# First FFN of a diffusion layer: up product once over 1280 tokens in chunks of 512, 512 and 256, the gated features by way of DRAM to a down product in two blocks

## The chip, the cores and the metric

The kernel runs on one core of one Trainium2 chip. The metric is the device time of one execution in microseconds (us). TensorE (PE in the profile; PEld is its weight load) multiplies, VectorE (DVE) and ScalarE (ACT) do elementwise work, GpSimd (POOL) does nearly nothing here, and SyncE (SP) issues the transfers between DRAM and the on-chip memory (SBUF).

## The reference

One layer over 1024 latent and 256 context tokens, width 1024: a half-step SwiGLU FFN, a mixer (neighbourhood attention and a state-space scan, S5), and a second half-step FFN. The change is in the first FFN, which both token streams go through with the same weights:

```python
mod = jnp.split((jax.nn.silu(c) @ w_ada[layer] + b_ada[layer])[:, None, :], 9, axis=-1)
...
def swiglu(h, w_up, w_down):
    a, g = jnp.split(h @ w_up, 2, axis=-1)
    return (jax.nn.silu(g) * a) @ w_down
...
x = post_norm(x, 0.5 * mod[2] * swiglu(modulate(x, mod[0], mod[1]), ffn1_w_up[layer], ffn1_w_down[layer]),
              ln_g[layer, 0], ln_b[layer, 0])
h_c = post_norm(h_c, 0.5 * mod_c[2] * swiglu(modulate(h_c, mod_c[0], mod_c[1]),
                                             ffn1_w_up[layer], ffn1_w_down[layer]),
                ln_g[layer, 0], ln_b[layer, 0])
```

D_FF is 2816, that is 22 features of 128 (the code's `NF`); the up weights are 44 units (a and g for each feature), the down weights 22.

## The kernel before

Each product keeps float32 accuracy by splitting both operands into a high part that TensorE takes exactly and a rest. `mm3` (L337 to L339) then makes three matmuls of one: high by high, high by low, low by high. Weights are loaded as 512 KB units (`ws`, L221), and each half of a unit is split by ACT (`wh`, L259) and DVE (`wl`, L261) into a ring of four.

The first FFN takes the 1280 tokens in two blocks of 640, b = 0 and 1, the second half latent and half context (384 latent, 256 context). Each block is done in two halves h of 11 features. In a half `ffn_up` makes the 11 hidden features: for each unit `by_feature` runs over two chunks of tokens, 384 and 256, with eight k-steps of three matmuls in each, into a PSUM bank per chunk. `gate` multiplies a by silu(g) (L365 silu on ACT, L366 product on DVE) and splits the result into high (L367) and low (L368, put off to the next `flush`). The hidden features stay in SBUF (`HA`, `HB`). `token_major` then makes the down product: features by five token tiles by three matmuls of 512 columns (L397 to L399), twice for the two halves of the output's 1024 columns; its `evac` adds the result, times a gate row, to the residual tile (L610, L611). So the up and the down weights are loaded and split once for each block.

The head of the program loads the modulation weights, builds the modulated input `X` (high and low, L526) eight k-slices one after the other, and `grow` already computes the first four units on each slice as it comes in. After a block the layer norm runs: statistics (L420), scaling (L436), and a store of each normed tile to a DRAM array, `xh` (L624), which `xm_a` later reads back (`z`, L1008) and transposes on TensorE (L450) as input of the mixer. For block 0 this transposing lies in the up and down products of block 1.

The order within an engine is that in which the program issues. `pump` lets generators of side work (preparation of S5, the modulation rest `mods_rest`, normed rows) advance a few us at a time between products. SP issues its transfers strictly in order, so one that has to wait holds back those behind it.

Of the kernel before, what the change touches and what calls it, by code (L numbers as in the profile page):

```python
# [38 lines left out]
NHX = 2368  # L39
TAIL = 8  # L40
# [8 lines left out]
def hybrid_layer(ctx: ExitStack, tc: tile.TileContext, I, out, dbg=None, stop=99):  # L49
# [67 lines left out]
    def ztile():  # L117
        return work.tile([128, 1024], F32, name=nm("z"), tag="z", bufs=4)
# [19 lines left out]
    ffn = lambda i: [I[f"w{p}{i}"][h * n + j] for h in range(2) for p, n in (("u", NF), ("d", NF // 2)) for j in range(n)]  # L138
# [52 lines left out]
    plain(ffn(1) * 2 + col("wu", 4) + wv[:2] + col("wu", 4) + wv[2:] + wv)  # L191
# [8 lines left out]
    for f, i in ORDER:  # L200
        item(*sv[f][i])
    DOWN = len(items)
    plain(col("wd2", NF) + [I["wd2"][f:f + 2, :, h * 512:(h + 1) * 512].rearrange("f p c -> p f c")
                            for h in range(2) for f in range(0, NF, 2)])
# [90 lines left out]
    early = slott("HA", [128, 16 * NB])  # L295
    mod_room = [early[:, i * 1024:(i + 1) * 1024] for i in range(10)]
# [72 lines left out]

    def ffn_up(X, chunks, hid, us, started=()):  # L370
        part = lambda f, c: [hid(i, f)[:, chunks[c][0]:sum(chunks[c])] for i in range(2)]
        for f, (a, g) in enumerate(started):
            for c in range(len(chunks)):
                flush()
                gate(a[c], g[c], *part(f, c))
        for f in range(len(started), NF // 2):
            a = by_feature(take(2), X, chunks, "m", lambda c, p: (pump(us), flush()))
            by_feature(take(2), X, chunks, "m", lambda c, p: (pump(us), flush(), gate(a[c], p, *part(f, c))))
        flush()
# [104 lines left out]
    def x_block(m=KD, n=NB):  # L484
# [3 lines left out]
    CH = ((0, 384), (384, 256))  # L488
    X = x_block()
    room = slott("HX", [128, NHX], F32R)  # L490
    room = [slott(f"A{i}", [128, 1024], F32R) for i in range(5)] + [room[:, 0:1024], room[:, 1024:2048],
                                                                   rowt().bitcast(F32R)]
    for i in range(8):
        apart[i] = room[i][:, 0:512], room[i][:, 512:1024]
    pb8 = [[bank("s")[:, :n] for _, n in CH] for _ in range(4)]
# [12 lines left out]
    for k in range(KD):  # L508
# [16 lines left out]
        S.activation(X[0][k], xt, AF.Copy)  # L525
        rest_of = lambda k=k, xt=xt: V.tensor_tensor(X[1][k], xt, X[0][k].bitcast(F32), op=ALU.subtract)  # L526
# [16 lines left out]
    def mods_rest():  # L543
        todo = [(m, k, lat, cx) for m, lat, cx in
                ((2, 1, 1), (0, 0, 1), (1, 0, 1), (3, 1, 1), (4, 1, 1), (5, 1, 0), (6, 1, 0), (7, 1, 0), (8, 1, 0))
                for k in range(KD)]
        hx = slott("HX", [128, NHX])
        mod_room[:] = [xe[:, 2, :], xe[:, 3, :], hx[:, 0:1024], hx[:, 1024:2048]]
        ws = [mod_load(*t[:2]) for t in todo[:4]]
        yield None  # L550
        for i, (m, k, lat, cx) in enumerate(todo):
            mod_tile(ws.pop(0), m, k, lat, cx)
            if i + 4 < len(todo):
                ws.append(mod_load(*todo[i + 4][:2]))
            yield 1.35 * (lat + cx)
            if (m, k) == (2, KD - 1):
# [6 lines left out]
        V.tensor_tensor(modc[:, 0:2, :], modc[:, 0:2, :], bada[:, 0:2, :], op=ALU.add)  # L563
# [12 lines left out]
    def x_build(X):  # L576
        for k in range(0, KD, 2):
            zs = [ztile()[:, 0:NB] for i in range(2)]
            for i in range(2):
                dq.dma_start(zs[i], I["xT"][k + i, :, NB:2 * NB])  # L580
            yield None
            yield None
            for i in range(2):
                j = k + i
                z = zs[i]
                S.activation(z[:, 0:384], z[:, 0:384], AF.Identity, scale=modl[:, 1, j:j + 1], bias=modl[:, 0, j:j + 1])
                S.activation(z[:, 384:NB], z[:, 384:NB], AF.Identity, scale=modc[:, 1, j:j + 1],
                             bias=modc[:, 0, j:j + 1])
                split(X[0][j], X[1][j], z)
                yield 0.8  # L590


    def ffn(X, chunks, zs, gates, us, done, last=None, scale=1.0, affine=None, started=()):
        N = chunks[-1][0] + chunks[-1][1]
        nt = N // 128
        for h in range(2):
            ha, hb = slott("HA", [128, 16 * NB], F32R), slott("HB", [128, 6 * NB], F32R)

            def hid(i, f):
                n = i * (NF // 2) + f  # L600
                t, n = (ha, n) if n < 16 else (hb, n - 16)
                return t[:, n * N:(n + 1) * N]

            ffn_up(X, chunks, hid, us[0], started if h == 0 else ())
            if h == 1 and last is not None:
                last()

            def evac(hf, t, p):
                z = zs[t][:, hf * 512:(hf + 1) * 512]
                V.tensor_tensor(p, p, gates(t)[:, hf * 512:(hf + 1) * 512], op=ALU.mult)  # L610
                V.scalar_tensor_tensor(z, z, scale if h == 0 else 1.0, p, op0=ALU.mult, op1=ALU.add)  # L611
                if h:
                    half_done(t, hf, z)

            half_done, rest = norm(affine)
            token_major(NF // 2, nt, lambda f, t: (hid(0, f)[:, t * 128:(t + 1) * 128],
                                                   hid(1, f)[:, t * 128:(t + 1) * 128]), evac, us[1],
                        (2, 2) if h == 0 or affine is None else (2, TAIL))
        if affine is None:
            hi.append(rest(zs, done))  # L620
# [397 lines left out]
    zn = []  # L1018
    hi.append(rows_in(zn, I["xt"], 5))
    for b in range(2):  # L1020
        zs, zn = zn, []

        def nxt():
            if b == 0:
                Xn.append(x_block())
                hi.append(x_build(Xn[0]))
            else:
                drain(bg)
                hi.append(xm_a())

        Xn = []
        ffn(X, CH, zs, lambda t: rows["g2c" if b == 1 and t >= 3 else "g2"], ((2.2, 2.4), (2.4, 2.4))[b], ln1_done(5 * b),
            last=nxt, scale=ALPHA, started=started if b == 0 else ())
        if b == 0:
            hi.append(rows_in(zn, I["xt"][5:10], 5))
            X = Xn[0]
# [791 lines left out]
def layout(inp):  # L1828
# [15 lines left out]
    for i in (1, 2):  # L1844
        w = a[f"ffn{i}_w_up"][0].reshape(KD, 128, 2, NF, 128)
        r[f"wu{i}"] = asc(w.transpose(3, 2, 1, 0, 4).reshape(2 * NF, 128, 1024))
        w = a[f"ffn{i}_w_down"][0].reshape(2, NF // 2, 128, 2, 512).transpose(0, 3, 1, 2, 4)
        r[f"wd{i}"] = asc(w.reshape(NF, 2, 128, 512).transpose(0, 2, 1, 3).reshape(NF, 128, 1024))
    r["wd2"] = asc(a["ffn2_w_down"][0].reshape(NF, 128, 1024))
# [49 lines left out]
```

## Time and profile before

| what | value |
| --- | --- |
| median of three runs | 2208.72 us (2207.69 to 2210.64) |
| the profiled execution: its own time, its span | 2211.69 us, 2209.6 us |
| mean granted TensorE clock | 0.994 |
| PE busy | 2154.9 us (98%) |
| DVE busy | 1597.0 us (72%) |
| ACT busy | 739.1 us (33%) |
| bytes moved | 372.31 MB, mean 169 GB/s |

The profile is of one execution, and its own time is 3.0 us above the median. The first FFN takes about the first 967 us of the span. "Granted clock" is the share of TensorE's full clock that the chip allowed it.

### The profile page before, as it was taken

The numbers are of one execution on the slowest core, as the hardware profiler recorded it, in microseconds if no ns is written. First come the engines' busy times: TensorE is split into PE (matmuls) and PEld (weight loads), VectorE is DVE, ScalarE is ACT, GpSimd is POOL, SyncE is SP. The second block draws the span as 40 slices with busy tenths as digits, with TensorE's granted clock in tenths as the row PEclk, the third lists the DMA queues.
The fourth block names the chain that finished last, engine by engine and source line by source line (L and its number), as shares of the span: only waits on it lengthen the run. The fifth ranks groups of instructions, "written<-read, shape, count | busy, mean of one in ns | idle before, by whom it ended". The sixth has DMA issues, their size and how long they took to land. (4 is left out here: it accounts for less than half of the span.)

```text
span 2209.6 us, 32479 instructions
## 1 busy us (share of the span) xinstructions
PE 2154.9 (98%) x12272; PEld 1933.3 (87%) x12272; DVE 1597.0 (72%) x3425; ACT 739.1 (33%) x1547; POOL 22.0 (1%) x33
## 2 busy tenths in 40 slices
PE   6999999999999999999999999999899999999998
PEld 6998899889998999898899899986688888888786
DVE  7888878798887887553777466788877777744845
ACT  4322223423322223324222367634433333332121
POOL 0000000000000000000000000000000000000000
PEclk9999999999999999999999999999999999999999
DMA  9787723436433444433877675244223333279442
GB/s 353 251 291 258 268 67 109 161 100 237 128 124 117 126 135 128 137 125 128 274 252 248 179 175 136 81 168 162 103 108 114 115 114 115 96 266 390 168 150 83
DMA packets 169612, 372.31 MB, mean 169 GB/s; under 512 B 18152, under 2 KB 85736, under 8 KB 166640
## 3 DMA queue, kind: packets, MB, share of 16 engines
q1 hardware_dynamic: 169456, 370.25, 49.6%
q8 instruction: 96, 1.57, 0.3%
q14 instruction: 60, 0.49, 0.1%
HBM read 292.09 MB, written 84.06 MB: 170 GB/s over the span
## 5 line engine op out<-in xcount | busy, mean ns | idle before, releaser
L337 PE MATMUL pb<-X,wh 128*128 128x256 f32 (+2 forms) x1744 | 558.2, 320 | 0.9 <-ACT wh L259 0.9
L339 PE MATMUL pb<-X,wl 128*128 128x256 f32 (+2 forms) x1744 | 555.8, 319 | 0.0
L261 DVE TENSOR_TENSOR wl<-ws,wh 128x512 fp32r<-128x512 f32 x456 | 304.1, 688 | 246.8 <-ACT wh L259 241.3
L259 ACT ACTIVATE wh<-ws 128x512 fp32r<-128x512 f32 x456 | 278.7, 627 | 563.3 <-PE pb L399 288.0
L337 PEld LDWEIGHTS pb<-X,wh 128*128 128x128 f32 x1744 | 330.7, 190 | 9.6 <-ACT wh L259 1.3
L339 PEld LDWEIGHTS pb<-X,wl 128*128 128x128 f32 x1744 | 330.4, 189 | 8.7 <-DVE wl L261 0.4
L338 PE MATMUL pb<-X,wh 128*128 128x256 f32 (+2 forms) x946 | 306.8, 324 | 0.0
L338 PE MATMUL pb<-XT,wh 128*128 128x256 f32 (+2 forms) x886 | 283.3, 320 | 0.9 <-DVE XT L134 0.9
L397 PE MATMUL pb<-wh,HA 128*128 128x512 f32 x592 | 232.4, 393 | 2.0 <-DVE hid L366 1.4
L398 PE MATMUL pb<-wl,HA 128*128 128x512 f32 x592 | 230.5, 389 | 0.8 <-DVE wl L261 0.8
L338 PEld LDWEIGHTS pb<-X,wh 128*128 128x128 f32 x946 | 179.1, 189 | 7.1
L338 PEld LDWEIGHTS pb<-XT,wh 128*128 128x128 f32 x886 | 168.1, 190 | 6.4 <-DVE XT L134 1.8
L337 PE MATMUL pb<-HA,wh 128*128 128x512 f32 (+2 forms) x424 | 154.1, 364 | 0.6 <-ACT wh L259 0.6
L339 PE MATMUL pb<-HA,wl 128*128 128x512 f32 (+2 forms) x424 | 153.0, 361 | 0.0
L1642 DVE TENSOR_TENSOR z<-pb,z 128x512 f32<-128x512 f32 x154 | 106.1, 690 | 47.2 <-PE pb L339 43.8
L397 PEld LDWEIGHTS pb<-wh,HA 128*128 128x128 f32 x592 | 111.2, 188 | 26.0 <-DVE hid L366 2.3
L398 PEld LDWEIGHTS pb<-wl,HA 128*128 128x128 f32 x592 | 111.2, 188 | 23.5 <-DVE wl L261 1.2
L399 PE MATMUL pb<-wh,HA 128*128 128x512 f32 x336 | 130.9, 389 | 0.0
L338 PE MATMUL pb<-HA,wh 128*128 128x512 f32 (+2 forms) x336 | 118.7, 353 | 0.0
L399 PE MATMUL pb<-wh,HB 128*128 128x512 f32 x252 | 98.1, 389 | 0.0
L337 PEld LDWEIGHTS pb<-HA,wh 128*128 128x128 f32 x424 | 79.8, 188 | 11.5 <-ACT wh L259 1.1
L339 PEld LDWEIGHTS pb<-HA,wl 128*128 128x128 f32 x424 | 79.8, 188 | 10.6 <-DVE wl L261 0.4
(465 smaller groups left out, 3776.9 us busy)
## 6 DMA issues: line engine op xcount, KB each, us to landing
ws<-wu SPq DMA_DIRECT2D x122, 512.0 KB
ws<-wd SPq DMA_DIRECT2D x88, 512.0 KB
hd<-XE SPq DMA_DIRECT2D x22, 1024.0 KB
XE<-wada SPq DMA_DIRECT2D x36, 512.0 KB
HX<-wada SPq DMA_DIRECT2D x36, 512.0 KB
XE<-s5m SPq DMA_DIRECT2D x21, 768.0 KB
HA<-hd SPq DMA_DIRECT2D x20, 512.0 KB
HX<-wu SPq DMA_DIRECT2D x18, 512.0 KB
```

The source lines that it names most:

```text
L259: S.activation(wh, src, AF.Copy)
L261: V.tensor_tensor(wl, ready.pop(i), wh.bitcast(F32), op=ALU.subtract)
L337: mm(p, lhsT=wh, rhs=xh, start=first, stop=False)
L338: mm(p, lhsT=wh, rhs=xl, start=False, stop=False)
L339: mm(p, lhsT=wl, rhs=xh, start=False, stop=last)
L397: mm(b[t], lhsT=h, rhs=wh, start=f + i == 0, stop=False)
L398: mm(b[t], lhsT=h, rhs=wl, start=False, stop=False)
L399: mm(b[t], lhsT=l, rhs=wh, start=False, stop=f + i == nf - 1)
L1642: V.tensor_tensor(o, s[i][0], x, op=ALU.add)
```

## The change

The up product of the first FFN is done once, for all 1280 tokens in three chunks (512, 512, 256), so that each of the 44 units is loaded and split once. The input `X` is now 16 tiles of 1280 columns in three SBUF regions, `HA` among them, so there is no room for the hidden features: `gate_out` stages the high and low part of each chunk in one of five `A` tiles and stores it to a DRAM array `h1d` of that feature. The down product then runs in two blocks of 640 tokens, over all 22 features at a time, and `hid_need` loads the hidden features of a block (655 KB for a feature) back into a ring eight steps ahead. There is one `evac` instead of two for each tile and output half.

The context part of `X` can't be built in the head. So the first five features (`NLAT`) are done for the latent chunks only, and their context chunk comes at the end of the up product, for which their ten units are loaded and split again. In the head the loads of x are 1024 instead of 640 columns, and the modulation weights go through six instead of ten tiles. The transposing `xm_a` of block 0 is now queued at the start of the down product of block 1.

```diff
-    plain(ffn(1) * 2 + col("wu", 4) + wv[:2] + col("wu", 4) + wv[2:] + wv)
+    plain(up1 + up1[:2 * NLAT] + down(1) * 2 + col("wu", 4) + wv[:2] + col("wu", 4) + wv[2:] + wv)
...
-    mod_room = [early[:, i * 1024:(i + 1) * 1024] for i in range(10)]
+    hx = slott("HX", [128, NHX])
+    mod_room = [xe[:, 2, :], xe[:, 3, :], hx[:, 0:1024], hx[:, 1024:2048], rowt(), rowt()]
...
-        x = ztile()[:, 0:NB]
-        dq.dma_start(x, I["xT"][k, :, 0:NB])
+        x = ztile()
+        dq.dma_start(x, I["xT"][k, :, 0:T])
...
-    CH = ((0, 384), (384, 256))
+    CH = ((0, 512), (512, 512), (1024, 256))
...
+    hd1 = [dram.tile([128, 2, NT], F32, name=f"h1d{f}") for f in range(NF)]
+    staged = [0]
+
+    def gate_out(f, c, a, g):
+        c0, n = CH[c]
+        w = stage[staged[0] % len(stage)]
+        staged[0] += 1
+        h, l = w[:, 0:n], w[:, n:2 * n]
+        gate(a, g, h, l)
+        sub.append(lambda: dq.dma_start(hd1[f][:, :, c0:c0 + n],
+                                        w[:, 0:2 * n].bitcast(F32).rearrange("p (i t) -> p i t", i=2)))
+
+    def up_first():
+        lat, cx = ((0, CH[0]), (1, CH[1])), ((2, CH[2]),)
+
+        def unit_pair(f, cs, us):
+            ch = [c for _, c in cs]
+            a = by_feature(take(2), X, ch, "m", lambda c, p: (pump(us), flush()))
+            by_feature(take(2), X, ch, "m", lambda c, p: (pump(us), flush(), gate_out(f, cs[c][0], a[c], p)))
...
+        for f in range(len(started), NF):
+            if f == NLAT:
+                while not ready_c:
+                    next(bg[0])
+            unit_pair(f, lat if f < NLAT else lat + cx, 3.2)
+        for f in range(NLAT):
+            unit_pair(f, cx, 0.8)
+        flush()
...
+    ring = rHA[3:8] + rHB + rHA[0:3]
+    seq += [ring[i % 11] for i in range(2 * NF)]
+    AHEAD = 8
+    loaded, now, used = [0], [-1], {}
+
+    def hid_need(n):
+        while loaded[0] < min(n + 1, 4 * NF):
+            i = loaded[0]
+            for j in range(i):
+                assert seq[j] is not seq[i] or j < now[0], (i, j)
+            b, f = i // (2 * NF), i % NF
+            dq.dma_start(seq[i].bitcast(F32).rearrange("p (i t) -> p i t", i=2), hd1[f][:, :, b * NB:(b + 1) * NB])
+            loaded[0] += 1
...
+    hid_need(2)
     for b in range(2):
...
+        if b == 1:
+            zs = zn
+            hi.append(xm_a())
+        half_done, rest = norm()
...
+        token_major(NF, 5, hidden1, evac, 2.4)
+        hi.append(rest(zs, ln1_done(5 * b)))
```

**From the up product to the down product.** In the kernel before, at the end of the first half's up product (b = 0, h = 0), TensorE's rows are the last of `mm3` (`X` by `wl`) and then the first down matmul, whose hidden feature `HA` lies in SBUF:

```order
L338 MATMUL pb_1789<-XT_109,wh_1687 128x256
L339 MATMUL pb_1789<-X_108,wl_1688 128x256
L397 MATMUL pb_1823<-wh_1747,HA_446 128x512 [waits Activation_49]
L398 MATMUL pb_1823<-wl_1748,HA_446 128x512 [waits DVE_49]
```

There the first down matmul waits for ACT alone. In the change the same place, now the end of the whole up product, reads so (the high part of feature 0's hidden tile is in `HB_5664`):

```order
L339 MATMUL pb_5625<-HA_112,wh_5582 128x256
L340 MATMUL pb_5625<-HA_112,wh_5582 128x256
L341 MATMUL pb_5625<-HA_112,wl_5583 128x256
L388 MATMUL pb_5668<-wh_5615,HB_5664 128x512 [waits DMAHW4_49,Activation_49]
L389 MATMUL pb_5668<-wl_5616,HB_5664 128x512 [waits DVE_49]
```

The wait for a transfer (`DMAHW4`) is new. SP's queue at that place in the change holds the store of the last staged chunk (`h1d_445` from `A_14_114`, 256 tokens of feature 4) and behind it the loads of hidden features 0, 1 and so on, all for 640 tokens:

```order
L597 DMA h1d_444<-A_18_118 256x1x256 [waits DMAHW0_49,DVE_49,Activation_49]
L223 DMA ws_5623<-wd 128x2x512 [waits DMAHW1_49,Activation_49]
L869 DMA s5m<-HX_2791 128x4x128 [waits DMAHW2_49]
L597 DMA h1d_445<-A_14_114 256x1x256 [waits DMAHW3_49,DVE_49]
L1038 DMA HB_5664<-h1d_441 128x2x640 [waits DMAHW4_49,PE_49]
L1038 DMA HB_5664<-h1d_442 128x2x640 [waits DMAHW5_49]
L1038 DMA HB_5664<-h1d_443 128x2x640 [waits DMAHW6_49]
L223 DMA ws_5681<-wd 128x2x512 [waits DMAHW7_49]
L1038 DMA X_110<-h1d_444 128x2x640 [waits DMAHW0_49,PE_49]
```

So the first load that the down product needs stands behind a store that waits for the last low part from DVE.

**From block 0 to block 1 of the down product.** In the kernel before, the read-back of three normed tiles stands on SP far behind their stores, 170 rows later, in the second half of block 1:

```order
L221 DMA ws_9199<-wd 128x1024 [waits DMAHW1_49,DVE_49]
L1008 DMA z_9218<-xh_106 128x1024 [waits DMAHW2_49]
L1008 DMA z_9219<-xh_106 128x1024 [waits DMAHW3_49]
L1008 DMA z_9220<-xh_106 128x1024 [waits DMAHW4_49]
```

In the change SP's rows from the start of block 1 on hold the stores of the five normed tiles (`xh_108` from the `A` tiles), weight and hidden loads, and then the same three reads:

```order
L623 DMA xh_108<-A_625_5704 128x1024 [waits DMAHW0_49,DVE_49]
L623 DMA xh_108<-A_630_5732 128x1024 [waits DMAHW1_49,DVE_49]
L223 DMA ws_7140<-wd 128x2x512 [waits DMAHW2_49,Activation_49]
L1038 DMA HA_112<-h1d_451 128x2x640 [waits DMAHW3_49,PE_49]
L623 DMA xh_108<-A_634_5756 128x1024 [waits DMAHW4_49,DVE_49]
L1038 DMA HA_112<-h1d_452 128x2x640 [waits DMAHW5_49,PE_49]
L623 DMA xh_108<-A_639_5794 128x1024 [waits DMAHW6_49,DVE_49]
L623 DMA xh_108<-A_644_5825 128x1024 [waits DMAHW7_49,DVE_49]
...
L1038 DMA HA_112<-h1d_453 128x2x640 [waits DMAHW1_49,PE_49]
L999 DMA A_835_7206<-xt 128x1024 [waits DMAHW2_49]
L1007 DMA z_7210<-xh_108 128x1024 [waits DMAHW3_49]
L1007 DMA z_7211<-xh_108 128x1024 [waits DMAHW4_49]
L1007 DMA z_7212<-xh_108 128x1024 [waits DMAHW5_49]
```

Stores and reads are now in one stretch (the row left out is one more weight load). On TensorE the transposes of these three tiles come in the change after seven steps, of 15 matmuls each, of block 1:

```order
L388 MATMUL pb_7060<-wh_7160,HB_5664 128x512
L389 MATMUL pb_7060<-wl_7161,HB_5664 128x512
L390 MATMUL pb_7060<-wh_7160,HB_5664 128x512
L441 MATMUL pb_7268<-ident,z_7210 128x128 [waits DMAHW3_49,PE_49]
L441 MATMUL pb_7268<-ident,z_7211 128x128 [waits DMAHW4_49]
L441 MATMUL pb_7268<-ident,z_7212 128x128 [waits DMAHW5_49]
```

What moved is the distance: seven steps of TensorE's work lie between the end of block 0 and the transposes.

## Rows read from the trace of the kernel before

**Rows 1.** The page's first part: busy time, share, instructions.

```profile
PE 2154.9 (98%) x12272; PEld 1933.3 (87%) x12272; DVE 1597.0 (72%) x3425; ACT 739.1 (33%) x1547; POOL 22.0 (1%) x33
```

**Rows 2.** Windows: length, busy time of PE, PEld, DVE, ACT, POOL; PEclk, DMA share, GB/s.

```profile
49.00:967.00 918.00, 914.50 (x5605) 852.65 (x5604) 721.41 (x1750) 267.13 (x510) 3.27 (x5) 1.00 0.49 164
```

**Rows 3.** Waits of PE, 45 to 967 us: us in total, times, longest.

```profile
PE pb L397 <- DVE hid L366: 1.4, 1, 1.4
PE pb L450 <- DMA z<-xh: 1.0, 1, 1.0
...
PE pb L450 <- DVE hid L451: 0.2, 1, 0.2
```

**Rows 4.** Timeline of PE in an up product: start, us, engine and line.

```profile
149.87 0.34 PE L337 MATMUL pb<-X,wh 128*128 128x384 f32 x1
...
154.04 0.28 PE L337 MATMUL pb<-X,wh 128*128 128x256 f32 x1
...
156.91 0.34 PE L337 MATMUL pb<-X,wh 128*128 128x384 f32 x1
```

**Rows 5.** Timeline of PE in a down product, two starts 24 matmuls apart.

```profile
200.19 0.39 PE L397 MATMUL pb<-wh,HA 128*128 128x512 f32 x1
...
205.63 0.39 PE L397 MATMUL pb<-wh,HA 128*128 128x512 f32 x1
```

**Rows 6.** Waits of PE in the head, 0 to 49 us.

```profile
PE pb L338 <- DVE X L526: 4.9, 2, 2.5
```

**Rows 7.** Windows in the head.

```profile
15.00:20.00 5.00, 2.57 (x7) 1.85 (x8) 4.84 (x9) 3.00 (x6) 0.00 (x0) 1.00 1.02 405
```

**Rows 8.** Groups of DVE by shape, 49 to 967 us: count, busy us, mean ns.

```profile
L261 DVE TENSOR_TENSOR wl<-ws,wh 128x512 fp32r<-128x512 f32 x254 | 167.9, 688 | 104.8 <-ACT wh L259 104.2
L333 DVE SCALAR_TENSOR_TENSOR row<-HX,XE 128x1024 f32<-128x1024 f32 x48 | 58.6, 1222 | 3.9 <-DMA HX<-wada 3.2
...
L366 DVE TENSOR_TENSOR hid<-pb,hid 128x256 f32<-128x256 f32 x44 | 18.5, 420 | 8.2 <-ACT hid L365 8.0
...
L368 DVE TENSOR_TENSOR HB<-hid,HA 128x256 fp32r<-128x256 f32 x24 | 10.1, 419 | 1.9 <-ACT HA L367 1.9
```

**Rows 9.** Groups of ACT by shape, 49 to 967 us.

```profile
L367 ACT ACTIVATE HA<-hid 128x256 fp32r<-128x256 f32 x44 | 18.4, 418 | 49.9 <-DVE hid L366 49.9
L365 ACT ACTIVATE hid<-pb 128x256 f32<-128x256 f32 x44 | 16.8, 381 | 28.8 <-PE pb L339 28.5
```

**Rows 10.** Timeline of SP's queue: a 512 KB load with nothing else in flight.

```profile
293.57 0.33 SPq L221 DMA_DIRECT2D ws<-wu  x1
```

**Rows 11.** Windows behind that issue.

```profile
294.50:295.00 0.50, 0.50 (x6) 0.50 (x5) 0.43 (x3) 0.19 (x1) 0.00 (x0) 1.00 0.96 229
...
296.00:296.50 0.50, 0.50 (x7) 0.50 (x6) 0.50 (x3) 0.00 (x0) 0.00 (x0) 1.00 0.26 98
296.50:297.00 0.50, 0.50 (x6) 0.50 (x6) 0.43 (x4) 0.36 (x1) 0.00 (x0) 1.00 0.00 0
```

**Rows 12.** Windows in the second FFN, while its hidden features are loaded back.

```profile
1990.00:2000.00 10.00, 10.00 (x46) 8.29 (x45) 1.87 (x4) 2.10 (x4) 0.00 (x0) 1.00 1.04 398
```

**Rows 13.** Timeline of PE at block 0's end: the last down matmul.

```profile
488.24 0.39 PE L399 MATMUL pb<-wh,HB 128*128 128x512 f32 x1
```

**Rows 14.** Timeline of DVE behind it: norm statistics.

```profile
490.00 3.06 DVE L420 BATCH_NORM_STATS2 st<-A 128x6 f32<-128x512 f32 x5
```

**Rows 15.** Timeline of SP's queue behind it: the stores of the normed tiles.

```profile
496.53 2.46 SPq L624 DMA_DIRECT2D xh<-A  x3
```

**Rows 16.** Timeline of PE in the mixer, behind a wait for a transfer.

```profile
1264.89 0.35 PE L1302 MATMUL pb<-HB,HX 128*128 128x256 f32 x1 [2.23 <-DMA HB<-kd]
...
1267.63 0.63 PE L337 MATMUL pb<-X,wh 128*128 128x512 f32 x1
...
1272.65 0.39 PE L337 MATMUL pb<-X,wh 128*128 128x512 f32 x1
```

**Rows 17.** Windows of the same stretch.

```profile
1262.00:1272.00 10.00, 6.58 (x21) 5.20 (x21) 2.33 (x7) 2.03 (x3) 0.00 (x0) 0.68 1.06 305
```

More of the change, by code (lines that the diff above doesn't have):

```diff
@@ L39 @@
 NHX = 2368
+NLAT = 5
 TAIL = 8
@@ L202, in hybrid_layer @@
     DOWN = len(items)
-    plain(col("wd2", NF) + [I["wd2"][f:f + 2, :, h * 512:(h + 1) * 512].rearrange("f p c -> p f c")
-                            for h in range(2) for f in range(0, NF, 2)])
+    plain(col("wd2", NF) + down(2))
     def w_next(margin):
@@ L574, in mods_rest, with x_ctx @@
         yield 2
[L576 to L580, printed above, removed]
+    ready_c = []
+    def x_ctx():
+        for k in range(0, KD, 4):
+            z = ztile()
+            z4 = z.rearrange("p (k t) -> p k t", k=4)
+            dq.dma_start(z4, I["xT"][k:k + 4, :, T:NT].rearrange("k p t -> p k t"))
             yield None
-            yield None
-            for i in range(2):
+            for i in range(4):
@@ L584, in x_build @@
                 j = k + i
[L585 to L620, printed above, removed]
@@ L1016, in xm_a @@
         yield from rows_x(3, range(3, 5))
-    zn = []
-    hi.append(rows_in(zn, I["xt"], 5))
-    for b in range(2):
[L1021 to L1033, printed above, removed]
+    up_first()
@@ new lines, in hybrid_layer @@
+    tiles_of = lambda t, n: [t[:, i * NT:(i + 1) * NT] for i in range(n)]
+    hb1 = slott("HB", [128, 6 * NB], F32R)
+    rHB, rX, rXT, rHA = tiles_of(hb1, 3), tiles_of(xa, 6), tiles_of(xb_, 2), tiles_of(xc, 8)
+    seq = (rHB + rX + rXT + rHA) * 2 + rHB + rHA[0:3]
+    assert len(seq) == 2 * 19 + 6
+    seq = seq[:2 * NF] if len(seq) >= 2 * NF else seq
+    ring = rHA[3:8] + rHB + rHA[0:3]
+    seq += [ring[i % 11] for i in range(2 * NF)]
+    AHEAD = 8
+    loaded, now, used = [0], [-1], {}
@@ new lines, in hid_need, with hidden1, evac @@
+    def hid_need(n):
[6 more added lines that the diff above has]
+            loaded[0] += 1
+    zs = []
+    hi.append(rows_in(zs, I["xt"], 5))
+    hid_need(2)
+    for b in range(2):
+        if b == 1:
+            zs = zn
+            hi.append(xm_a())
+        half_done, rest = norm()
+        base_n = 2 * NF * b
+        def hidden1(f, t):
+            if t == 0 and (f > used.get("f", -1) or f == 0):
+                now[0] += 1
+                used["f"] = f if f < NF - 1 else -1
+                hid_need(now[0] + AHEAD)
+            v = seq[base_n + (NF if used.get("hf") else 0) + f].rearrange("p (i t) -> p i t", i=2)
+            return [v[:, i, t * 128:(t + 1) * 128] for i in range(2)]
+        def evac(hf, t, p):
+            z = zs[t][:, hf * 512:(hf + 1) * 512]
+            g = rows["g2c" if b == 1 and t >= 3 else "g2"]
+            V.tensor_tensor(p, p, g[:, hf * 512:(hf + 1) * 512], op=ALU.mult)
+            V.scalar_tensor_tensor(z, z, ALPHA, p, op0=ALU.mult, op1=ALU.add)
+            half_done(t, hf, z)
+            if t == 4:
+                used["hf"] = hf == 0
+        token_major(NF, 5, hidden1, evac, 2.4)
+        hi.append(rest(zs, ln1_done(5 * b)))
```

56 lines of the change are left out of this document (29 added, 27 removed).

## The prediction

> **What bounds the kernel now.** I read the page's busy shares first: PE is busy 98% of the span, DVE 72%, ACT 33% [rows 1]. That alone doesn't say that PE bounds the stage that is changed, so I took the stretch of the first FFN by itself: from 49 to 967 us PE is busy 914.5 of 918 us at a granted clock of 1.00, DVE 721 us, the transfers have 0.49 of their engines' time [rows 2]. So 3.5 us in all are not matmul there. The waits of PE in the stretch name most of it: 1.4 us where the first down product waits for hidden features, 1.2 us at the transposes [rows 3]. DVE and ACT have room. What a change is worth here is therefore: how many PE nanoseconds it removes, less the new places where PE has to wait. Relief for DVE and ACT is worth nothing as long as PE doesn't wait for them.
>
> **PE's own work.** Columns times contraction stay the same; only the chunks change. A unit's 24 matmuls of 384 columns start 4.17 us apart (149.87 to 154.04), the 24 of 256 columns 2.87 us [rows 4], 24 matmuls of 512 columns 5.44 us [rows 5]. Before, the up product is 44 units by two blocks by (4.17 + 2.87) = 619.5 us; after, 44 by (2 by 5.44 + 2.87) = 605.0 us. The difference is 14.5 us; it comes from 1056 matmuls fewer (one chunk of 24 less for each of 44 units: three instead of twice two). By pitch: 4.17/24 = 173.7 ns for 384 columns and 5.44/24 = 226.7 ns for 512, so 128 columns are worth 53 ns, and 13 to 14 ns of each matmul don't depend on the columns; 1056 by 13.3 ns is 14.0 us. I take **-14.0** (12.5 to 15, for starts are printed to 0.01 us). The down product keeps its matmuls.
>
> The Trainium skill, "TensorE: Matmul & The Clock Gate", section "Wait — 56ns, not 53.3ns?", gives the fixed part of a matmul at full clock as about 2.5 ns. By it the change would save an estimated 1056 by 2.5 = 2.6 us instead of 14, and the whole forecast would end some 11 us higher. The three pitches of this kernel agree with one another on 13 ns and not with the page, and the measurement decides; the page's figure as a rival gets under 1 in 100.
>
> **The head.** Each of the eight k-slices of x grows by 128 by 384 by 4 bytes = 0.20 MB. From 15 to 20 us the transfers are saturated at 405 GB/s, and PE is busy about half of it [rows 7], since it waits 4.9 us in two waits for the low part of X [rows 6]. So a slice comes 0.20/0.405 = 0.49 us later than the one before. PE runs without waits from the third slice on: 3 by 0.49 = **+1.5**. Lower bound 0 (more columns for each slice fill the waits), upper bound 8 by 0.49 = 3.9.
>
> **Up to down.** Before, the first down matmul waits 1.4 us for a hidden feature [rows 3]; that goes, **-1.4**. In its place the first hidden load stands on SP behind the store of the last staged chunk, and that store waits for DVE's last low part. Behind the last up matmul (256 columns) come silu 0.38 us, copy 0.42 us [rows 9], product 0.42 us, rest 0.42 us [rows 8]: 1.64, with some 0.1 us for each of five handoffs 2.2 us. Then the store is issued and behind it the load, 0.33 us apiece at the issue of [rows 10] (0.5 us taken for both parts of the larger form: 0.5). The load: a 512 KB unit issued at 293.57 with nothing else in flight moves its last bytes in the slice 296.0 to 296.5, at 98 GB/s there and 0 behind it [rows 11], so it has landed about 2.7 to 2.9 us after issue. 655 KB at 398 GB/s [rows 12] are another 0.14 MB, 0.35 us; with the semaphore 3.4 us. Sum 2.2 + 0.5 + 3.4 + 0.2 = **+6.3** during which PE stands. Lower bound 3.4 less what is hidden, if the load passed the store (2 us); upper 8, if the other loads share the transfer engines with the first one.
>
> After a wait of this kind PE comes back at half clock (1.2 of 2.4 GHz). The example is in the mixer: a wait of 2.23 us for a transfer ends at 1264.89, and the twelve matmuls of 512 columns from 1267.63 to 1272.65 take 5.02 us [rows 16] where twelve at 226.7 ns would take 2.72; the granted clock in the ten us around is 0.68 [rows 17]. That is 2.3 us lost. **+2.3** for each stall of that size; bounds 0 (a short wait as that at the first down product leaves it) and 3.4.
>
> **Block 1's transposes.** Before, the normed tiles of block 0 are stored long ahead of their reads. After, stores, loads and the three reads form one stretch on SP, and the transposes come after seven steps of block 1: 7 by 15 by 226.7 ns = 23.8 us [rows 5]. When are the three tiles there? The stores wait for the norm. Before, from the last down matmul of block 0 at 488.24 [rows 13] over the statistics from 490.00 [rows 14] to the first store's issue at 496.53 [rows 15] it is 8.3 us; DVE's work at that place is the same now. Up to then SP stands at that store and transfers only finish. From there to the third read 5 stores, 2 weight loads, 3 hidden loads (655 KB), one xt and 3 reads go out: 11 by 0.524 + 3 by 0.655 = 7.7 MB, at 398 GB/s [rows 12] 19.4 us, and about 1 us until the first bytes move. 8.3 + 19.4 + 1.0 = 28.7 against 23.8: PE waits 4.9 us, **+4.9**, and the half clock again **+2.3**. Bounds: 0 where the reads or stores run at once with others and the hidden loads come behind (then 23.8 covers it), 9 where each of them waits for a ring of outstanding transfers. What goes is the wait of the old transposes, **-1.2** [rows 3].
>
> Queued behind that stalled PE is the rest of the down product, and nothing else; its hidden loads only gain time by it. The second group of transposes needs two more reads, which are issued behind the first and have the seven steps of the next stretch; I give it nothing, with 2 us as upper bound.
>
> **Hidden or off the path.** 68 weight splits fewer (44 up units and their halves less the ten reloaded ones), each 0.69 us on DVE [rows 8], are 47 of DVE's 721 us [rows 2]; 20 evacuations fewer come on top. PE waited for neither, so 0. The price is 57.7 MB of loads and some 29 MB of stores more, in a stretch that has 0.49 of the engines' time used at 164 GB/s [rows 2]: over 900 us this is 95 GB/s more, against 398 that the engines give [rows 12]; hidden but for stretches of a few us. The late context chunks of five features have 2 by 2.87 us of PE per feature and reload 1 MB, 2.6 us of transfer: covered; **+1.0** for that phase and the new staging, bounds 0 and 3.
>
> **Sum.** -14.0 + 1.5 - 1.4 + 6.3 + 2.3 - 1.2 + 4.9 + 2.3 + 1.0 = +1.7 us, on the profiled execution's own 2211.69 us: 2213.4. That execution is 3.0 us above the median of the runs shown, so on the median 2210.4 us. A measurement of this kernel can tell 0.2%, 4.4 us, from no change: 2204.3 to 2213.1 is "same".
>
> **The rivals.** First, the reads of block 0's normed tiles land in time. For it speaks that weight loads and hidden loads are several steps ahead of their need, so that the engines might serve the stores and reads first; against it that SP is strictly in order and blocked for 8.3 us. Then 7.2 us go: 2203.2; if the wait of up to down is short too (2 us, no half clock), 2196.6. It decides at 23.8 us from block start to the third read. Chance 0.26, 2194 to 2204.
>
> Second, on the other side: the gate's place in the up product. A pair of units now fills three PSUM banks for a and three for g, six accumulators for the five banks that the code gives to this product; before it was two and two. The next unit's first matmul needs the bank of g's second chunk, which is freed only when DVE has made the product of it. From the end of that chunk to the need lie 2.87 us of PE (the 256-column chunk); the chain is silu and product of 512 columns, about twice those of rows 8 and 9, 1.6 us with handoffs, so 1.2 us are left. While preparation of the modulation runs, DVE has rows of 1.22 us [rows 8], and one of them in front of the product uses that up. If it makes PE wait 0.7 us in each of the 17 features that do three chunks, that is 12 us: 2222. For it: DVE is at 79% of the stretch [rows 2]; against it: its work is given out a piece at a time between products, and it has 68 splits less. Chance 0.15.
>
> Third, the same mechanisms cost more: the hidden ring can't keep up with the down product right behind the block switch, which needs 655 KB and half a weight unit each 3.4 us, 268 GB/s, while the backlog of 7.7 MB is being worked off: a second stall of 5 us, 2215 to 2220. Chance 0.17.
>
> **Chances.** My forecast, both stalls within their size, has 0.42: 2204 to 2213, the likeliest 2210.5. Faster by over 0.2%: 0.26. Slower: 0.15 + 0.17 = 0.32. The range takes in the middle of the first rival and all of the second: 2199 to 2222.
>
> **What would show it.** Up product: starts of units 5.44 + 5.44 + 2.87 us apart, without waits between; a wait of PE of about 6 us for a load of `h1d` at the first down matmul, with matmuls at half clock behind it; 28 to 29 us from the last down matmul of block 0 to the first transpose, 5 us of it a wait for `z`; PE's first continuous matmul 1 to 2 us later in the head. I am wrong if PE waits in the up product for `hid` or for banks (then DVE's order sets the pace), or if neither wait for transfers is there.

## The result, and the profile after

The changed kernel takes 2226.39 us (median of 5 runs, 2220.39 to 2230.36) where the kernel before takes 2208.72 (5 runs, 2207.69 to 2210.83): a ratio of 1.0072, with a 95% interval of 1.0051 to 1.0092. It is slower, by 17.7 us in the medians; the forecast was 2210.5, with 2222 as upper end. The profiled execution of the changed kernel took 2221.59 us, the lower part of its spread, and 9.9 us more than the profiled one of before (2211.69).

The page's first part and the waits of PE from 45 to 1000 us of the changed kernel (us in total, times, longest):

```profile
PE 2143.1 (97%) x11216; PEld 1836.8 (83%) x11216; DVE 1525.6 (69%) x3273; ACT 688.7 (31%) x1427; POOL 23.2 (1%) x33
```

```profile
PE pb L388 <- DMA HB<-h1d: 9.9, 1, 9.9
PE pb L441 <- DMA z<-xh: 6.9, 3, 5.3
PE pb L339 <- ACT wh L261: 3.7, 2, 3.1
PE pb L341 <- DVE wl L263: 2.5, 3, 2.1
PE pb L339 <- DVE hid L368: 0.3, 1, 0.3
```

PE is busy 11.8 us less than in [rows 1], DVE 71 us less, and still the end is later: before, PE waited 3.3 us in this part of the program ([rows 3] has the longest of these waits), and now it waits some 23 us. Two of the waits were forecast by name, `h1d` at the first down matmul and `z` at the transposes. The waits for `wh` and `wl`, 5.2 us of which lie in one place, were not.

The matmul saving is there. PE's timeline in the up product (starts of a chunk of 512, of 256, and of the next unit's first chunk):

```profile
228.67 0.39 PE L339 MATMUL pb<-X,wh 128*128 128x512 f32 x1
...
234.11 0.28 PE L339 MATMUL pb<-X,wh 128*128 128x256 f32 x1
...
236.98 0.40 PE L339 MATMUL pb<-X,wh 128*128 128x512 f32 x1
```

5.44 us and 2.87 us, as read from [rows 4, 5]. Counting every matmul up to the end of the first FFN by its undisturbed pitch, PE's own work there fell by 14.6 us. The last down matmul starts at 966.52 us before and at 980.77 after, 14.2 us later.

**The stall that was not forecast.** PE's timeline near 130 us, and behind it ACT's and SP's in the same stretch:

```profile
129.60 0.39 PE L341 MATMUL pb<-HA,wl 128*128 128x512 f32 x1
133.12 0.50 PE L339 MATMUL pb<-X,wh 128*128 128x512 f32 x1 [3.14 <-ACT wh L261]
133.46 0.52 PE L340 MATMUL pb<-X,wh 128*128 128x512 f32 x1
136.08 0.80 PE L341 MATMUL pb<-X,wl 128*128 128x512 f32 x1 [2.10 <-DVE wl L263]
136.67 0.63 PE L339 MATMUL pb<-X,wh 128*128 128x512 f32 x1
```

```profile
121.89 0.60 ACT L583 ACTIVATE z<-z,modc 128x256 f32<-128x256 f32 x1 [10.53 <-DMA z<-xT]
...
128.68 0.60 ACT L583 ACTIVATE z<-z,modc 128x256 f32<-128x256 f32 x1 [2.91 <-DMA z<-xT]
...
132.46 1.14 ACT L261 ACTIVATE wh<-ws 128x512 fp32r<-128x512 f32 x2
```

```profile
116.07 0.43 SPq L579 DMA_DIRECT2D z<-xT  x1
...
121.09 2.68 SPq L579 DMA_DIRECT2D z<-xT  x1
```

Read from PE backwards: it wants the high part of the next weights, which ACT makes at 132.46. That split stands in ACT's queue behind the making of the context input (L583), and ACT has stood there 10.5 us for the first load of the context tokens and 2.9 us for the second. SP issued these loads only at 116.07 and 121.09. So the engine that PE waits for was itself idle, in order behind a late load. In the window from 129 to 145 us PE is busy 10.8 of 16 us at a granted clock of 0.79.

In the kernel before, ACT makes the context part of the input together with latent tokens, during the first block's last down product, from 419 to 456 us. From 395 to 490 us it waits for no load of tokens at all. One of its rows there:

```profile
419.79 0.59 ACT L587 ACTIVATE z<-z,modc 128x256 f32<-128x256 f32 x1
```

The old generator of this work also gave up its turn twice between issuing the loads and using them, the new one once. Whether a second pause alone would have sufficed was not tested.

**From up to down.** PE, ACT, DVE and SP around the end of the up product:

```profile
648.97 0.28 PE L341 MATMUL pb<-HA,wl 128*128 128x256 f32 x1
659.19 0.77 PE L388 MATMUL pb<-wh,HB 128*128 128x512 f32 x1 [9.94 <-DMA HB<-h1d]
659.75 0.63 PE L389 MATMUL pb<-wl,HB 128*128 128x512 f32 x1
```

```profile
649.29 0.37 ACT L367 ACTIVATE hid<-pb 128x256 f32<-128x256 f32 x1
...
652.00 0.42 ACT L369 ACTIVATE A<-hid 128x256 fp32r<-128x256 f32 x1 [2.34 <-DVE hid L368]
```

```profile
648.90 1.29 DVE L263 TENSOR_TENSOR wl<-ws,wh 128x512 fp32r<-128x512 f32 x2 [1.92 <-PE pb L341]
650.17 0.17 DVE L872 MEMSET row<- 128x128 f32 x1
...
651.55 0.42 DVE L368 TENSOR_TENSOR hid<-pb,hid 128x256 f32<-128x256 f32 x1
...
652.45 0.42 DVE L370 TENSOR_TENSOR A<-hid,A 128x256 fp32r<-128x256 f32 x1 [0.48 <-ACT A L369]
```

```profile
652.90 0.52 SPq L597 DMA_DIRECT2D h1d<-A  x1
653.51 2.11 SPq L1038 DMA_DIRECT2D HB<-h1d  x3
```

The chain is the one of the forecast, link by link, but two links are longer. The silu ends at 649.66 and the product starts at 651.55: DVE is in a weight split until 650.19 and works off S5 rows behind it. And from the load's issue at 653.51 to its use at 659.19 it is 5.7 us, where 3.4 was put. The matmuls behind it take 0.63 us each: the granted clock is 0.50 from 653 to 660 us, the lower of its two levels (1.2 GHz).

**The transposes.** The end of block 0's down product, SP's stores and reads, and the transposes:

```profile
815.23 0.39 PE L390 MATMUL pb<-wh,HA 128*128 128x512 f32 x1
...
839.03 0.39 PE L390 MATMUL pb<-wh,HB 128*128 128x512 f32 x1
844.71 0.45 PE L441 MATMUL pb<-ident,z 128*128 128x128 f32 x1 [5.29 <-DMA z<-xh]
...
847.22 2.40 PE L441 MATMUL pb<-ident,z 128*128 128x128 f32 x10 [0.85 <-DMA z<-xh]
```

```profile
824.20 1.07 SPq L623 DMA_DIRECT2D xh<-A  x2
...
833.19 3.19 SPq L1007 DMA_DIRECT2D z<-xh  x3
```

From the last matmul of block 0 at 815.23 to the first store's issue it is 9.0 us (8.3 in [rows 13, 15]), to the first transpose 29.5 us and to that of the third tile 32.0 us, where the forecast said 28.7 to the third read. The three reads land one after the other, and PE waits for each, a further 0.74 and 0.85 us.

### The profile page after: what moved, and what is told of

It is laid out like the page before. It is cut to its first block, busy times and chain, and to the rows that moved or that the text cites. A ratio compares the mean times of both kernels' runs of the same rounds, so it can differ in the third digit from the quotient of the medians.

```text
span 2219.8 us, 30229 instructions
## 1 busy us (share of the span) xinstructions
PE 2143.1 (97%) x11216; PEld 1836.8 (83%) x11216; DVE 1525.6 (69%) x3273; ACT 688.7 (31%) x1427; POOL 23.2 (1%) x33
## 2 busy tenths in 40 slices
DMA packets 212130, 440.85 MB, mean 199 GB/s; under 512 B 19976, under 2 KB 94216, under 8 KB 209168
## 5 line engine op out<-in xcount | busy, mean ns | idle before, releaser
L339 PE MATMUL pb<-HA,wh 128*128 128x512 f32 (+2 forms) x920 | 328.5, 357 | 0.6 <-ACT wh L261 0.6
L341 PE MATMUL pb<-HA,wl 128*128 128x512 f32 (+2 forms) x920 | 327.3, 356 | 0.0
L340 PE MATMUL pb<-HA,wh 128*128 128x512 f32 (+2 forms) x832 | 293.0, 352 | 0.0
L339 PE MATMUL pb<-X,wh 128*128 128x512 f32 (+2 forms) x772 | 275.4, 357 | 5.0 <-ACT wh L261 4.6
L341 PE MATMUL pb<-X,wl 128*128 128x512 f32 (+2 forms) x772 | 272.9, 354 | 2.5 <-DVE wl L263 2.5
L340 PE MATMUL pb<-X,wh 128*128 128x512 f32 (+2 forms) x646 | 231.0, 358 | 0.0
L339 PEld LDWEIGHTS pb<-HA,wh 128*128 128x128 f32 x920 | 174.0, 189 | 24.0 <-ACT wh L261 1.0
L341 PEld LDWEIGHTS pb<-HA,wl 128*128 128x128 f32 x920 | 173.6, 189 | 23.2 <-DVE wl L263 0.4
L340 PEld LDWEIGHTS pb<-HA,wh 128*128 128x128 f32 x832 | 157.3, 189 | 19.4
L339 PEld LDWEIGHTS pb<-X,wh 128*128 128x128 f32 x772 | 146.5, 190 | 24.4 <-ACT wh L261 5.6
L341 PEld LDWEIGHTS pb<-X,wl 128*128 128x128 f32 x772 | 146.3, 190 | 22.2 <-DVE wl L263 4.1
L389 PE MATMUL pb<-wl,HA 128*128 128x512 f32 x407 | 158.5, 389 | 0.8 <-DVE wl L263 0.8
L340 PEld LDWEIGHTS pb<-X,wh 128*128 128x128 f32 x646 | 122.7, 190 | 16.5
L340 PE MATMUL pb<-XT,wh 128*128 128x512 f32 (+2 forms) x338 | 119.6, 354 | 0.9 <-DVE XT L135 0.9
```

Of the source, the lines that this page charges most:

```text
L339: mm(p, lhsT=wh, rhs=xh, start=first, stop=False)
L340: mm(p, lhsT=wh, rhs=xl, start=False, stop=False)
L341: mm(p, lhsT=wl, rhs=xh, start=False, stop=last)
L389: mm(b[t], lhsT=h, rhs=wl, start=False, stop=False)
```

## The experiments

In what follows "excess" is the sum, over a stretch, of the distances between the starts of PE's matmuls less an undisturbed matmul's pitch (226.6, 173.7, 119.6 ns for 512, 384, 256 columns, 109 ns for a transpose): waits and half clock together. The "end of the first FFN" is the start of its last down matmul in the profiled execution, 966.52 us in the kernel before and 980.77 in the changed one; it leaves out the spread of everything behind.

**Context loads earlier.** The two loads of the context tokens are issued after the third row of the modulation's scale, into a slot that is free then:

```diff
...
+            if (m, k) == (1, 2):
+                for q in range(2):
+                    dq.dma_start(zc[q], I["xT"][4 * q:4 * q + 4, :, T:NT].rearrange("k p t -> p k t"))
...
-            z = ztile()
-            z4 = z.rearrange("p (k t) -> p k t", k=4)
-            dq.dma_start(z4, I["xT"][k:k + 4, :, T:NT].rearrange("k p t -> p k t"))
+            z4 = zc[k // 4]
```

> The two loads of the context tokens are issued some 15 us earlier, into an unused slot; nothing else changes. Theory: the stall near 130 us in the changed kernel (waits of 3.1 us for a high weight part and 2.1 us for a low one, then matmuls at half clock) comes from ACT standing in order behind the context loads, with the weight splits queued behind it; so both waits go and the time falls by 3.1 + 2.1 + 2 to 3 us of half clock, 7 to 9 us, to about 2218. Rival: the splits are late because DVE and ACT have too much work there (modulation rows of 1.22 us); then the waits stay within 1 us of what they were and the time stays at 2220 to 2230.

Measured: 2219.08 us (2216.36 to 2220.82), ratio to the kernel before 1.0036 (1.0024 to 1.0049). The loads go out from 99.2 us on in place of 116.1 and 121.1. The trace of this run has no wait of PE at all from 100 to 145 us; the excess there is 0.03 us where the changed kernel has 7.9. The first FFN ends at 974.63 us, 6.1 earlier than in the changed kernel. ACT makes the whole context input without a wait, one split ahead of it and one behind:

```profile
112.69 1.14 ACT L261 ACTIVATE wh<-ws 128x512 fp32r<-128x512 f32 x2
113.73 0.59 ACT L586 ACTIVATE HB<-HB,modc 128x256 f32<-128x256 f32 x1
...
121.27 1.14 ACT L261 ACTIVATE wh<-ws 128x512 fp32r<-128x512 f32 x2
```

DVE and ACT have the same work as in the changed kernel (1525.9 and 689.0 us busy, there 1525.6 and 688.7), so the rival, too much work, falls.

**Six features without context first.**

```diff
-NLAT = 5
+NLAT = 6
```

> Six features in place of five are done for the latent chunks only (two more units loaded and split again). The context input then has one more feature's time, 22 us, and is made a piece at a time between products. Theory: the stall near 130 us is the context input being made in one go in front of the first feature that needs it, so it goes with this number alone: 7 us or so less. Rival: the stall is the load of DVE and ACT in that stretch; then it moves by a feature to about 150 us and stays.

Measured: 2231.47 us (2225.47 to 2233.01), slower than the changed kernel's 2226.68 on the same chip. Neither outcome came: the stall neither went nor moved. PE waits at the same place, and ACT for the same loads (waits of PE from 125 to 140 us, of ACT from 100 to 140 us):

```profile
PE pb L339 <- ACT wh L261: 2.6, 1, 2.6
PE pb L341 <- DVE wl L263: 2.2, 1, 2.2
```

```profile
ACT z L583 <- DMA z<-xT: 12.9, 2, 10.9
```

So it isn't the forced making of the context input in front of the feature that needs it (which now comes 22 us later); side work hands it to ACT at the same time anyway, and ACT stands in front of a load that is in flight. My theory's half about the late load holds, its half about the forced drain falls. Why the time rises stays open. Beside the rerun of the changed kernel (below), PE waits longer at the transposes (10.1 us in five waits from 825 to 880 us, 7.7 there) and less for `h1d` (8.1 us, 10.3 there); the first FFN ends 1.4 us later than in the rerun, and 3.5 us more come behind it.

**Hidden loads earlier.** The ring is set up, and the loads of features 0 to 2 are issued, before the last context chunk in place of after it:

```diff
         for f in range(NLAT):
+            if f == NLAT - 1:
+                hid_start()
+                hid_need(2)
             unit_pair(f, cx, 0.8)
...
-    hid_need(2)
     for b in range(2):
```

> The loads of the first three hidden features are issued before the last feature's context chunk, so ahead of the last two stores on SP. Theory: PE's wait of 9.9 us at the first down matmul is the chain silu, product, rest, store, load behind the last up matmul; with the first three loads ahead of it the wait is under 2 us and the half clock behind it goes, 10 to 12 us less, about 2215. Rival: the wait is transfer bandwidth (0.76 to 1.05 of the engines' time busy around it), then the fourth feature's load is as late as the first was, and PE waits 6 to 9 us for that one 10 us further on: 2220 or more.

Measured: 2218.65 us (2215.74 to 2221.97), ratio 1.0037 (1.0024 to 1.0049). Waits of PE from 640 to 680 us:

```profile
PE pb L388 <- DMA X<-h1d: 1.4, 1, 1.4
PE pb L388 <- DMA HB<-h1d: 0.8, 1, 0.8
```

9.9 us of wait became 0.8, and the fourth feature, whose load can't come earlier because its place holds the up product's input, costs 1.4. The order on SP was the cause; bandwidth has a small part. The time fell by 8 us, less than the 10 to 12 expected. The trace shows where the rest went: the excess from 600 to 685 us fell by 8.9 us, but from 685 to 825 us it rose by 2.1, with three waits of PE for the evacuation of its results (L1066, 1.1 us in all) that the changed kernel doesn't have. The first FFN ends at 973.83 us, 6.9 earlier.

**One hidden load earlier.** As above with `hid_need(0)` at that place and `hid_need(2)` where it was.

> Of the hidden loads only feature 0's is issued ahead of the last stores, features 1 and 2 behind them as in the changed kernel. Theory (the chain behind the last up matmul sets when loads can be issued): the first down step starts at once, and PE waits at the second, 3.4 us later, for about 9.9 - 3.4 = 6.5 us: 3 to 5 us less than the changed kernel. Rival (transfer bandwidth, the three loads share the engines): feature 1's load has fewer beside it and lands sooner, so the wait is under 4 us and 7 us or more are gained.

Measured: 2224.92 us (2219.59 to 2226.65), 1.8 us under the changed kernel on the same chip, less than either side expected; the first FFN ends at 977.55 us, 4.4 earlier than in the rerun. PE waits 1.2 us at the first step and, 3.4 us of work later, 4.1 us at the second, 5.2 in all. SP's issues of these loads, one early and two behind the last store, and PE's two waits:

```profile
644.03 0.59 SPq L1038 DMA_DIRECT2D HB<-h1d  x1
...
653.04 1.28 SPq L1038 DMA_DIRECT2D HB<-h1d  x2
```

```profile
650.30 0.47 PE L388 MATMUL pb<-wh,HB 128*128 128x512 f32 x1 [1.17 <-DMA HB<-h1d]
658.03 0.80 PE L388 MATMUL pb<-wh,HB 128*128 128x512 f32 x1 [4.06 <-DMA HB<-h1d]
```

The second wait is nearly the rival's in size. But the number of hidden loads that go out together doesn't set how long one takes: the load issued at 653.04 with one more was used 5.0 us later, the single one of 644.03 only 6.3 us later, and three together took 5.7 us in the changed kernel and 5.1 in the next run (647.19 to 652.28). What the run does show is that moving one load ahead of the last stores moves the wait from the first step to the second.

**No side work among the context chunks.**

```diff
-            unit_pair(f, cx, 0.8)
+            unit_pair(f, cx, 0.0)
```

> No side work (S5 preparation) is given out between the five context chunks at the end of the up product; it runs later in the same stage. Theory: of PE's 9.9 us wait at the first down matmul about 2 us are DVE's side work (649.66 to 651.55) ahead of the last product, so the wait falls to about 8 us and the rest (5.6 us of transfer behind 2.5 us of chain) stays: 2 us less, 2220 to 2226. Rival: the side work's stores also stood in the transfer queues ahead of the load; then the wait falls to 6 us, which is the sum that was predicted.

Measured: 2225.9 us (2224.16 to 2228.0), the same as the changed kernel. The link that it aimed at shrank as expected: the store is issued 2.1 us after the last matmul's start (646.62, 644.53) in place of 3.9, and the wait is 7.5 us. But the side work that was put off weighs on the later stage: PE waits from 640 to 880 us in this kernel:

```profile
PE pb L441 <- DMA z<-xh: 9.4, 4, 5.7
PE pb L388 <- DMA HB<-h1d: 7.5, 1, 7.5
PE pb L441 <- DMA HA<-h1d: 0.9, 1, 0.9
```

The transposes cost 9.4 us against 6.9 (7.7 in the rerun), so that the 2.4 us won at the first down matmul are given back there. How the put-off work brings that about was not traced further.

**Transposes later.** `xm_a` of block 0 is queued when the first output half of block 1 is done:

```diff
         if b == 1:
             zs = zn
-            hi.append(xm_a())
...
             if t == 4:
                 used["hf"] = hf == 0
+                if b == 1 and hf == 0:
+                    hi.append(xm_a())
```

> Reading back and transposing block 0's normed tiles is queued at the second output half of block 1 in place of its start. Theory: the waits for these tiles (5.3 us, and 1.1 and 1.3 us for the next two) come from stores and reads lying in one stretch of 24 us; half a block later the tiles are long in DRAM, the waits of 6.9 us and 2 to 3 us of half clock go: 9 us less, about 2217. Rival: the down product's loads fill the transfer engines anyway (357 GB/s and more over whole stretches), so the reads are as late at the later place: waits of 4 us or more remain there and the time is within 3 us of the changed kernel's.

Measured: 2219.27 us (2218.29 to 2223.76), ratio 1.0044 (1.0030 to 1.0058). The waits of PE for `z` from 800 to 980 us:

```profile
PE pb L441 <- DMA z<-xh: 2.5, 3, 0.9
```

6.9 us became 2.5, none over 0.9, and the first FFN ends at 975.17 us, 5.6 earlier. The reads themselves are no faster. SP's issue of them and the transpose of the second tile in this run:

```profile
892.08 1.52 SPq L1007 DMA_DIRECT2D z<-xh  x3
```

```profile
903.26 0.33 PE L441 MATMUL pb<-ident,z 128*128 128x128 f32 x1 [0.67 <-DMA z<-xh]
```

In the changed kernel the reads were issued at 833.19, behind stores that stood until 824.20, PE was ready for them 6.2 us later, and the first was there after 11.5 us. Here the stores are long done, and PE comes to the first tile 10.2 us after the reads' issue (902.32), so most of their time is hidden. The 2.5 us that stay fit the rival: the transfer engines are busy all the time here too (share 1.02 from 890 to 900 us and 1.08 from 900 to 910).

**All three.** The edits of the three kernels above together.

> All three edits together. Theory: the stalls are independent, so 8 + 11 + 9 = 28 us less than the changed kernel: 2226 - 28 = 2198, below the kernel before (2208.7) by about 10 us, which is the 14 us of matmul time saved less the head and small waits. Rival: the matmul saving isn't there in full or another wait takes the place of those removed: 2205 to 2215.

Measured: 2202.70 us (2201.94 to 2207.26), ratio 0.9967 (0.9955 to 0.9980): faster than both kernels. The three together are worth 23.7 us against the changed kernel's 2226.4, the single ones 7.3, 7.7 and 7.1, 22.1 in sum. The changed kernel was measured in another session, where the kernel before took 2208.72 us and not 2211.27 as here; by the ratios to it the single edits are worth 8.0, 7.7 and 6.2 us and all three 23.2, each uncertain by some 5 us (an estimate from the intervals). The ends of the first FFN agree: 6.1, 6.9 and 5.6 us earlier one by one, 19.2 together (961.54 us). So they add up. The sum stays short of the expected 28 us. The first FFN ends 5.0 us before that of the old kernel, not 14.6, since waits of up to 1.3 us each are left, among them in all 1.8 us for `z`, 1.3 for the product in the up product, 1.2 for the fourth hidden feature and 1.1 for evacuations. Run again:

> The version with all three edits once more, on the same chip as the one with halved chunks: 2202 to 2207, faster than the kernel before by 5 to 9 us. If the first result was chance, it is within 2 us of the kernel before.

Measured: 2205.75 us (2204.34 to 2209.12, 11 runs), ratio 0.9977 (0.9969 to 0.9986). So it is about 0.2 to 0.3% faster than before; the first FFN ends at 961.07 us here.

**The fixed part of a matmul.** On the version with all three edits, each first chunk of 512 columns is made as two halves in the same bank:

```diff
...
-                mm3(p, wh[:, s], wl[:, s], X[0][k][:, c0:c0 + n], X[1][k][:, c0:c0 + n], k == 0, k == KD - 1)
+                for o in ((0, 256) if cut and c0 == 0 else (0,)):
+                    m = 256 if cut and c0 == 0 else n
+                    mm3(p[:, o:o + m], wh[:, s], wl[:, s], X[0][k][:, c0 + o:c0 + o + m],
+                        X[1][k][:, c0 + o:c0 + o + m], k == 0 and o == 0, k == KD - 1 and o + m == n)
...
```

> The version with all three edits, with the matmuls of each first chunk of 512 columns (20 features, two units each) made as two of 256 into the same bank: 960 matmuls more for the same columns, weights, splits and gates. The fixed part of a matmul read from the pitches (226.7 and 119.6 ns) is 2 by 119.6 - 226.7 = 12.5 ns, so 960 by 12.5 = 12.0 us more than the version without: about 2215. Rival, the fixed part of about 2.5 ns that the Trainium skill states (TensorE: Matmul & The Clock Gate, section Wait - 56ns, not 53.3ns?): by it an estimated 2.4 us more, about 2205.

Measured: 2217.76 us (2214.26 to 2221.32, 12 runs) against 2205.75 on the same chip: 12.0 us for 960 matmuls, 12.5 ns each. PE's timeline: the start of a context chunk, of the next unit's first chunk in halves, and of its second chunk:

```profile
230.53 0.28 PE L339 MATMUL pb<-X,wh 128*128 128x256 f32 x1
...
233.40 0.28 PE L339 MATMUL pb<-X,wh 128*128 128x256 f32 x1
...
239.16 0.40 PE L339 MATMUL pb<-X,wh 128*128 128x512 f32 x1
```

The 24 matmuls of the context chunk take 2.87 us and the 48 of the halves 5.76, where 24 of 512 columns take 5.44. The Trainium skill's figure of about 2.5 ns ("TensorE: Matmul & The Clock Gate", section "Wait — 56ns, not 53.3ns?") gives an estimated 2.4 us here; the measured 12.0 us decides against it for this kernel's matmuls. The profiled executions agree: with the halves the first FFN ends 10.4 us later (971.50, 961.07) and has 1.5 us less excess, 11.9 us in all. That the medians, of runs spread over 5 to 7 us, hit 12.0 to the tenth is luck.

**The changed kernel again.** Unaltered.

> The changed kernel once more, unaltered, on the same chip as the next three. Theory: the same three stalls at the same places with 8, 12 and 10 us above the matmuls' own time, and a time of 2220 to 2230. Rival for the spread of its runs: one stall is much longer in some executions; then this profile shows one of the three off by more than 3 us from the first.

Measured: 2226.68 us (2225.2 to 2228.08). The same three stalls, with waits of 2.6 and 2.2 us for weights, 10.3 us for `h1d` and 7.7 us for `z`. They differ by under a microsecond each from the first profile, so no single stall explains the difference between the two. The first FFN ends at 981.98 us, 1.2 later than in the first profile.

## Why the prediction was wrong, point by point

The terms of its sum, beside the excess of the two profiled executions in the same stretches:

| term | predicted | measured |
| --- | --- | --- |
| fewer matmuls | -14.0 | -14.6 by count; 12.5 ns each in the test with halves |
| head | +1.5 | +0.1 (8.4 of excess from a start at 12.61, before 9.1 from 11.86) |
| up to down, wait of before taken off | -1.4 + 6.3 + 2.3 = +7.2 | 11.8 - 1.8 = +10.0 |
| transposes, wait of before taken off | -1.2 + 4.9 + 2.3 = +6.0 | 9.3 - 2.1 = +7.2 |
| late context chunks and staging | +1.0 | +1.8 |
| making the context input | nothing | +7.9 |
| sum | +1.7 | +12.4, of 14.2 at the end of the first FFN |

Of the 16.0 us by which the median missed the forecast, 12.5 are found in the first FFN of the profiled execution (14.2 less the forecast 1.7).

**The step that failed** is the one that called the rest "Hidden or off the path" and priced "that phase and the new staging" at 1.0 us. It looked at the late context chunks' PE time and weight loads, and not at the context input itself, which the change moves from the first block's last down product into the middle of the up product, as ACT work behind two loads. That term was put at nothing without a reason. The text listed what is queued behind the stalled PE at the transposes, but it never asked what is queued on ACT behind these loads: the weight splits, which PE needs within one unit's time. The term measured 7.9 us, and the run with early context loads, where they are gone, shows their cause. With this term alone put right the sum would have been 2218.3 us, inside the stated range.

**Mis-sized** is the step from up to down: the mechanism, its place and its order were right, but two links were priced as if the engines were free. Between silu and product lie 1.9 us, 0.5 of them a weight split and the rest S5 rows; without side work the store came 1.8 us sooner. (The 0.1 us put for each handoff was too much: 0.03 to 0.04 us lie between one link's end and the next one's start where nothing else is in the way.) The load took 5.7 us from issue to use, against 3.4 worked out from a load with nothing else in flight [rows 10, 11]; the upper bound of 8 us for the whole wait was passed. The transposes came out 1.2 us dearer than forecast.

**Right** are the matmuls' fixed part, the mechanism at the block switch (28.7 us forecast to the third read, 32.0 measured to its transpose) and the half clock behind each stall: 2.3 us were put, and the excess beyond the waits is 2.7, 1.9 and 2.4 us at the three stalls. The example from which the 2.3 us were read is less clear than it was told. The granted clock is still 1.00 from 1264 to 1265 us, when the wait of 2.23 us has just ended; PE then makes one matmul and waits another 1.18 us; the granted clock is 0.67 from 1265 to 1267 and 0.50 from 1267 to 1270. The head cost +0.1 us, near its lower bound. That relief for DVE and ACT is worth nothing was not tested by itself. DVE lost 71 us of work; of the 3.3 us of waits before, the 1.4 us at the first down matmul went, a place that the change rebuilt, and 0.5 us for evacuations, which may be relief. The count of the new traffic left out the 34 units of up weights that are no longer loaded, 17.8 MB; the page has 68.5 MB more in all (440.85 and 372.31), which changes nothing in the sum.

The first rival, reads that land in time, didn't come: SP stood until 824.20, and the third transpose came 32.0 us behind block 0's end, not 23.8. The second, the gates in five banks, didn't either: PE waits 0.3 us for the product in the whole up product. The third, a hidden ring that can't keep up behind the block switch, didn't come: from 664 to 838 us PE is busy all 174 us, and no later wait for `h1d` is in the changed kernel's list. It was the nearest in time (2215 to 2220), but the stall that came on top lies elsewhere and has another cause.

**What stays open.** The medians are 17.7 us apart, the profiled executions 9.9. Behind the first FFN the profiled changed kernel took 1239.0 us and the one of before 1243.0, in code that is the same. This is spread: two profiles of the kernel with all three edits have 1239.3 and 1243.7 us there, the rerun of the changed kernel 1241.5, the run with six features 1244.9. So the small distance of the two profiled executions was luck. What makes this spread was not traced, and 3.5 of the 16.0 us have no place.

## What to carry to other kernels

When a product is reordered so that its inputs or results pass through DRAM, write down for every new load which engine waits for it in order, and what that engine has queued behind: an idle engine in front of a load stops the busiest one as surely as an overloaded one. Three stalls of 8 to 12 us shrank to waits of 0 to 2.5 us when loads were issued 9 to 21 us earlier, or reads and their use placed some 60 us later, without any change of the work. Price a link of such a chain by rows from a busy stretch, not from a lone transfer or an idle queue.

## What was not expected of the hardware

A 655 KB load among other transfers was used 5.0 to 6.3 us after its issue by a TensorE that stood waiting for it (5.7 us in the changed kernel, 5.1 without side work, 5.0 and 6.3 in the run with one early load), and the number of such loads issued together didn't order these times; a lone 512 KB load had needed under 3 us [rows 10, 11]. No run has a hidden load with nothing else in flight, so how much of the difference the other transfers make and how much the load's own form stays open. And some 12.5 ns of each matmul don't depend on its columns: 960 matmuls more for the same columns cost 12.0 us.
